# Pairs of tiles behind the early ones in three mixers, alternating pieces in the recurrent mixer, and pieces set apart from their chains

## The chip, the cores and the metric

The kernel runs on one core of one Trainium2 chip. Times are device microseconds (us) of one execution; several are taken and the median counts. Engines: PE is TensorE, DVE VectorE, ACT ScalarE, POOL GpSimd, SP the engine that issues the loads.

## The reference

A sequence of 256 tokens with 1024 features goes through six layers, in float32. The first two are hybrid layers: an input projection `w_in`, then three token mixers side by side (retention with rotated q and k, gated linear attention "gla" with its q called gq, and softmax attention with normalised q and k, "fox": fq, fk, fv), gated and summed, then a feed-forward part with a short convolution. The last four have one mixer each and a feed-forward part, with a normalisation behind each part. All norms are modulated by vectors from a condition `c` (scale, shift, gate: products of `c` with 288 blocks of 128 x 1024 weights).

```
def hybrid_layer(x, c_act, ...):
    h = modulate(rms_norm(x, norm1_g), shift1, scale1)
    (rq, rk, rv, rg, gq, gk, gv, glr, gg, fq, fk, fv, ff) = jnp.split(h @ w_in, split_points, axis=-1)
    ...
def second_block(x, c, ...):
    for i in range(4):
        h = x * (1 + scale[0]) + shift[0]
        y = (mlstm_mixer, swa_mixer, hgrn2_mixer, diff_mixer)[i](h, ...)
        x = layer_norm(alpha * x + (1 + gate[0]) * y, ...)
        h = x * (1 + scale[1]) + shift[1]
        x = layer_norm(alpha * x + (1 + gate[1]) * swiglu(h, ...), ...)
```

swa is attention in a window of 128 with 16 query heads of 64 and two key heads; hgrn2 a gated recurrence with 8 heads of 128; diff attention takes the difference of two softmaxes in each of 8 heads and then a norm over each head.

## The kernel before

Activations lie transposed: eight tiles x0 to x7 of 128 features by 256 tokens. Every weight block (128 x 128) and every activation tile is split into a rounded high part and a low part, and three matmuls (high by high, high by low, low by high) make one block product: lines L501 to L503 (`mm3`, 256 columns, output transposed) or L508 to L510 (`mm3n`, output in token order, up to 512 columns wide). These are called dense matmuls here. SP loads weights in pieces of 128 x 1024 in the order of use; for each, ACT makes the high part (the cast, L469) and DVE the low part (L470).

The list of matrices (`dense_specs`) sets what is multiplied in which order: `tiles` for `dense_T`, `chunks` for `dense_N`. In `dense_T` the first `group` output tiles, the early ones, run over k in step, while the norm of the layer before isn't finished: they use unnormalised inputs, and `fix` corrects their sums (L799 to L803) once the norm is known. The functions in `after` then make the normed inputs x0 to x7 (in the last layers three DVE operations, L1402, L1404, L1407, and one of ACT each). `evac(f, tile)` takes a finished tile out of PSUM and may push pieces: a list `fill` of short functions (scores, softmax, transposes, values of one head and so on), of which one or more run behind each dense tile (`step`; `mid` says how often inside one). `late` puts a piece behind a wait for a chain; a chain is an inverse square root on POOL (L653 to L664, L839). `held` pieces are kept back. What is issued to an engine stays in that order.

Where the matrices have a `second` number of tiles (up and fi, the feed-forward parts: groups of six, two pairs), these run behind the early tiles as pairs, again over k in step, and the inputs are made in two parts: x0 to x5, two fixes and evacuations, x6 and x7, the other fixes and evacuations.

Stages that the text names: up0, down0 (feed-forward of the first layer), rk1, gs1, fq1, fk1, fv1, gv1, gq1, rv1, rq1 (projections of the second hybrid layer), ml_* (mLSTM), sw_in and sw_w (sliding window), hg_qf0, hg_v, hg_qf1, hg_g, hg_w (hgrn), df_kq0, df_v0, df_kq1, df_v1, df_w (diff). `RATES` says how many modulation blocks are loaded by SP and summed by DVE (L415) per dense tile of a stage.

In hgrn the heads are worked in four pairs of twelve pieces each: `first` and five levels (L1799, matmuls of 32 x 32), three wide ones (L1842, L1852, L1857), `heads` (L1869 to L1871) with a chain on POOL, an empty one and `done`. In diff, heads 0 to 3 have pieces at once and 4 to 7 are held until the second half of the values exists; the piece `done` normalises a head and transposes it (L823).

## Time and profile before

| what | value |
|---|---|
| median of three runs | 2310.58 us (2307.93 to 2315.93) |
| profiled execution | 2307.1 us, span 2305.3 us |
| TensorE busy | 2198.5 us, 95% |
| VectorE busy | 1879.3 us, 82% |
| ScalarE busy | 1249.3 us, 54% |
| GpSimd busy | 104.8 us, 5% |
| mean granted TensorE clock | 0.981 of full speed |

The stages run one behind the other on PE. Busy time of PE contains overlap of matmuls in its pipeline, so a stretch is read by the idle time before an instruction and what ended it. The chain of work that ended last is PE for 48% and issue on PE for 36% of the span.

### The profile page before, as it was taken

How to read it: one execution, taken by the hardware profiler on the slowest of the kernel's cores; microseconds unless marked ns; L12 is line 12 of the kernel's file. 1: busy time of each engine (PE TensorE's matmuls, PEld its weight loads, DVE VectorE, ACT ScalarE, POOL GpSimd, SP SyncE). 2: the span in 40 equal slices, each digit the busy share in tenths (PEclk: the TensorE clock that was granted, in tenths of full speed). 3: DMA queues.
4: the chain of work that ended last, by engine and by line, in shares of the span. 5: the costliest groups of instructions: out<-in, count | busy, mean ns of one | idle time of the engine just before them, and what ended most of it. 6: DMA issues, size and time to landing. Idle time of an engine off the chain costs nothing.

```text
span 2305.3 us, 46019 instructions
## 1 busy us (share of the span) xinstructions
PE 2198.5 (95%) x17991; PEld 2104.0 (91%) x17991; DVE 1879.3 (82%) x3624; ACT 1249.3 (54%) x2426; POOL 104.8 (5%) x280
## 2 busy tenths in 40 slices
PE   6999999998999999989999999999989999889997
PEld 5899999996899999979999879998879999779997
DVE  8879898877877888847998869887769987968855
ACT  3545475454554665456644576445655544576542
POOL 0011000002020000002000000000010000030000
PEclk9999999999999999999999999999999999899998
DMA  9759858856777578945699325984545896444751
GB/s 358 254 177 341 280 197 266 310 190 235 254 250 274 186 249 276 328 151 174 209 374 324 109 92 170 326 308 156 170 135 173 310 317 212 140 132 144 258 184 34
DMA packets 144939, 520.26 MB, mean 226 GB/s; under 512 B 16208, under 2 KB 18512, under 8 KB 144720
## 3 DMA queue, kind: packets, MB, share of 16 engines
q1 hardware_dynamic: 144432, 517.15, 65.6%
q8 instruction: 141, 2.31, 0.4%
q14 instruction: 78, 0.64, 0.1%
q10 hardware_dynamic: 288, 0.16, 0.0%
HBM read 516.20 MB, written 1.05 MB: 224 GB/s over the span
## 4 chain that ended last, share of the span: by engine, by line
PE 48%; issue 36%; DVE 8%; POOL 3%; ACT 2%; DMA 2%; SPq 0%; POOLq 0%; ACTq 0%; DVEq 0%
PE dps L501 13%; PE dps L502 13%; PE dps L503 13%; DVE l L470 2%; POOL nr L656 2%; DMA w<-in_ada_dram 1%; PE dps L509 1%; PE dps L510 1%; PE dps L508 1%; DVE junk L415 1%; ACT h L469 1%; DVE t L1407 1%; PE mps L502 1%; ACT t L882 1%; PE mps L503 1%
## 5 line engine op out<-in xcount | busy, mean ns | idle before, releaser
L501 PE MATMUL dps<-t,h 128*128 128x256 f32 (+1 forms) x4664 | 1325.1, 285 | 6.9 <-DVE t L1259 3.2
L502 PE MATMUL dps<-t,h 128*128 128x256 f32 (+1 forms) x4664 | 1318.7, 283 | 2.1 <-DVE t L491 2.0
L503 PE MATMUL dps<-t,l 128*128 128x256 f32 (+1 forms) x4664 | 1315.3, 283 | 2.0 <-DVE l L470 2.0
L469 ACT CAST h<-w 128x1024 fp32r<-128x1024 f32 x689 | 718.2, 1047 | 627.6 <-PE dps L502 338.2
L470 DVE TENSOR_TENSOR l<-w,h 128x1024 fp32r<-128x1024 f32 x689 | 832.9, 1216 | 179.9 <-ACT h L469 175.4
L501 PEld LDWEIGHTS dps<-t,h 128*128 128x128 f32 x4664 | 883.4, 190 | 12.5 <-issue 6.5
L503 PEld LDWEIGHTS dps<-t,l 128*128 128x128 f32 x4664 | 885.2, 190 | 4.7 <-DVE l L470 2.9
L502 PEld LDWEIGHTS dps<-t,h 128*128 128x128 f32 x4664 | 884.6, 190 | 4.5 <-DVE t L491 2.6
L415 DVE SCALAR_TENSOR_TENSOR junk<-w,cb 128x1024 bf16<-128x1024 f32 x288 | 350.8, 1218 | 52.2 <-DMA w<-in_ada_dram 44.7
L508 PE MATMUL dps<-h,t 128*128 128x512 f32 (+2 forms) x288 | 107.6, 385 | 15.5 <-ACT t L882 6.1
L509 PE MATMUL dps<-l,t 128*128 128x512 f32 (+2 forms) x288 | 108.2, 381 | 4.7 <-DVE l L470 4.5
L510 PE MATMUL dps<-h,t 128*128 128x512 f32 (+2 forms) x288 | 106.8, 380 | 0.0
L490 ACT CAST t<-t 128x256 fp32r<-128x256 f32 x172 | 68.1, 403 | 58.4 <-DVE t L1265 25.8
L839 POOL TENSOR_SCALAR nr<-nr 128x2 f32<-128x2 f32 (+2 forms) x22 | 13.7, 624 | 1587.7 <-ACT junk L882 1544.8
L508 PEld LDWEIGHTS dps<-h,t 128*128 128x128 f32 x288 | 57.6, 201 | 28.6 <-ACT t L882 9.2
L502 PE MATMUL mps<-t,h 128*128 128x256 f32 (+1 forms) x288 | 81.0, 284 | 1.7 <-DVE t L1407 1.7
L501 PE MATMUL mps<-t,h 128*128 128x256 f32 (+1 forms) x288 | 80.2, 285 | 1.1 <-ACT t L882 1.1
L503 PE MATMUL mps<-t,l 128*128 128x256 f32 (+1 forms) x288 | 80.3, 284 | 0.9 <-DVE l L470 0.9
L491 DVE TENSOR_TENSOR t<-t,t 128x256 fp32r<-128x256 f32 x172 | 70.4, 417 | 5.9 <-ACT t L490 5.9
L509 PEld LDWEIGHTS dps<-l,t 128*128 128x128 f32 x288 | 57.7, 201 | 15.1 <-DVE l L470 7.3
L510 PEld LDWEIGHTS dps<-h,t 128*128 128x128 f32 x288 | 57.2, 201 | 8.8 <-issue 0.3
L502 PEld LDWEIGHTS mps<-t,h 128*128 128x128 f32 x288 | 54.4, 189 | 2.3 <-DVE t L1407 2.3
(387 smaller groups left out, 2075.4 us busy)
## 6 DMA issues: line engine op xcount, KB each, us to landing
w<-in_w_dram SPq DMA_DIRECT2D x683, 512.0 KB, 4.6
w<-in_ada_dram SPq DMA_DIRECT2D x288, 512.0 KB, 5.0
w<-in_w_dram SPq DMA_DIRECT2D x4, 414.0 KB, 4.1
t<-in_c_dram SPq DMA_DIRECT2D x4, 256.0 KB, 4.4
X<-in_x_dram SPq DMA_DIRECT2D x8, 128.0 KB, 3.6
v<-in_ret_dram SPq DMA_DIRECT2D x2, 512.0 KB, 7.7
out_dram<-X SPq DMA_DIRECT2D x8, 128.0 KB, 2.0
cols<-in_cols_dram SPq DMA_DIRECT2D x1, 740.0 KB, 6.8
```

What stands on the lines that cost most here:

```text
L415: self.nc.vector.scalar_tensor_tensor(out=self.junk, in0=w, scalar=0.5, in1=self.cb, op0=ALU.mult, op1=ALU.mult, accum_out=self.mod[l][:, ...
L469: nc.scalar.copy(h[:, q:e], raw[:, q:e]).ins,
L470: nc.vector.tensor_tensor(out=low[:, q:e], in0=raw[:, q:e], in1=h[:, q:e].bitcast(F32), op=ALU.subtract).ins]
L490: nc.scalar.copy(t[:, 0], src)
L491: nc.vector.tensor_tensor(out=t[:, 1], in0=src, in1=t[:, 0].bitcast(F32), op=ALU.subtract)
L501: mm(pt, lhsT=h, rhs=x[:, 0], start=first, stop=False)
L502: mm(pt, lhsT=h, rhs=x[:, 1], start=False, stop=False)
L503: self.last_mm = mm(pt, lhsT=low, rhs=x[:, 0], start=False, stop=last).ins
L508: mm(pt, lhsT=x[:, 0, sl], rhs=h, start=first, stop=False)
L509: mm(pt, lhsT=x[:, 0, sl], rhs=low, start=False, stop=False)
L510: self.last_mm = mm(pt, lhsT=x[:, 1, sl], rhs=h, start=False, stop=last).ins
L656: e.tensor_tensor(out=o, in0=a, in1=b, op=ALU.mult)
```

## The change

In the list of matrices, three mixers get a pair behind their four early tiles: rk1 takes gq1's two tiles as its pair (gq1's own stage goes), hg_qf0 and df_kq0 have six tiles instead of four (hg_qf1 and df_kq1 ten instead of twelve). In `dense_T` the two branches on the group's size become branches on `second`, and the `elif not norm` becomes `else`. In hgrn the pieces of a new pair of heads alternate with the last eight in the list; `gated` goes to the front of the list from the fourth tile of hg_g. In diff `done` is divided: the normalisation, and a stage later `rows` with the transposes; three heads are pushed at once. In mLSTM two transposes become a piece of their own (`as_columns`), and three empty pieces stand in front of the first head. In the second hybrid layer the normalisation pieces of q and k come two pieces later. Of the rates, up0 goes from 0.32 to 0.5, down from 3 to 2.2 (down0 to 2).

```diff
-            tiles(f"rk{l}", 8, 4, cols(slice(RK, RK + 512)))
+            tiles(f"rk{l}", 8, 6, cols(list(range(RK, RK + 512)) + list(range(GQ, GQ + 256))), 4, 2)
...
-    tiles("hg_qf0", 8, 4, lambda i: qf(i)[:, :512])
+    tiles("hg_qf0", 8, 6, lambda i: qf(i)[:, :768], 4, 2)
...
-    tiles("df_kq0", 8, 4, lambda i: kq(i)[:, :512])
+    tiles("df_kq0", 8, 6, lambda i: kq(i)[:, :768], 4, 2)
...
-RATES = dict(..., up0=0.32, down=3, ...
+RATES = dict(..., up0=0.5, down=2.2, down0=2, ...
...
-                if group == 4:
+                if not s["second"]:
                     xs = []
                     for f in range(group):
                         pts[f] = norm["fix"](pts[f])
                         xs += [t() for t in after[2 * f:2 * f + 2]]
                     for f in range(group):
                         evac(f, pts[f])
-            if norm and group > 4:
+            if norm and s["second"]:
                 xs = [t() for t in after[:6]]
                 self.fixes(norm, [0, 1], pts, evac)
                 xs += [t() for t in after[6:]]
                 self.fixes(norm, range(2, group), pts, evac)
-            elif not norm:
+            else:
                 for f in range(group):
                     evac(f, pts[f])
...
-            rk, hx = rotated(f"rk{l}", norm)
+            hx = self.dense_T(f"rk{l}", norm, lambda f, pt: ev_k(f, pt) if f < 4 else evac_gq(f - 4, pt))
...
-            self.fill += [norm_q]
+            self.fill += [lambda: None] * 2 + [norm_q]
...
-        self.fill = [lambda: None] * 3 + [lambda h=h: decay(h) for h in range(4)]
+        self.fill = [lambda: None, as_columns, lambda: None] + [lambda h=h: decay(h) for h in range(4)]
...
-                    self.fill += pieces(b)
+                    k = max(0, len(self.fill) - 8)
+                    new, alone, old = pieces(b), self.fill[:k], self.fill[k:]
+                    self.fill = alone + [p for a in zip(old, new) for p in a] + new[len(old):]
...
-        held, self.fill = self.fill[9:], self.fill[:9]
+        held, self.fill = self.fill[8:], self.fill[:8]
         self.dense_N("hg_v", hx, evac_v)
-        self.fill += held
-        self.mid = 2
+        self.drain()
+        self.fill = held
+        self.mid = 1
...
-            if f > 5:
-                gated()
+            if f > 2:
+                self.fill.insert(0, gated)
...
+        def rows(h, o):
+            t = o[0]
             out[h] = self.split(self.transposed(lambda th: t[:, th * 128:(th + 1) * 128]), lm[:, 3:4])
...
-            if h < 2:
+            if h < 3:
                 first.append(stages)
...
-        self.dense_N("df_v0", hx, evac_v)
+        self.fill = [lambda: None] * 3 + self.fill
+        self.dense_N("df_v0", hx, evac_v, 1)
```

Lines of the changed kernel lie 1 to 13 further down. DVE at the head of the differential mixer, before: the casts' low parts (l), the fix of the first two early tiles (L800, L802), and the inputs' operations (t2 is an input's low part).

```order
L470 TENSOR_TENSOR l_24593<-w_24590,h_24592 128x1024
L470 TENSOR_TENSOR l_24719<-w_24716,h_24718 128x1024
L470 TENSOR_TENSOR l_24725<-w_24722,h_24724 128x1024
L800 TENSOR_TENSOR t1_24621<-dps_24464,t2_24582 128x256
L1402 SCALAR_TENSOR_TENSOR t1_24627<-Z0_114,c4_23656,t2_24582 128x256
L802 SCALAR_TENSOR_TENSOR t1_24621<-t2_24582,nr_24620,t1_24621 128x256
L1404 SCALAR_TENSOR_TENSOR t1_24627<-t2_24582,c4_23656,t1_24627 128x256
L1402 SCALAR_TENSOR_TENSOR t1_24633<-Z1_115,c4_23656,t2_24582 128x256
L800 TENSOR_TENSOR t1_24639<-dps_24465,t2_24582 128x256
L1407 SCALAR_TENSOR_TENSOR t2_24626<-t1_24627,c4_23656,t2_24626 128x256
L1404 SCALAR_TENSOR_TENSOR t1_24633<-t2_24582,c4_23656,t1_24633 128x256
L802 SCALAR_TENSOR_TENSOR t1_24639<-t2_24582,nr_24638,t1_24639 128x256
```

The same place in the changed kernel:

```order
L471 TENSOR_TENSOR l_24712<-w_24709,h_24711 128x1024
L471 TENSOR_TENSOR l_24840<-w_24837,h_24839 128x1024
L1403 SCALAR_TENSOR_TENSOR t1_24740<-Z0_114,c4_23776,t2_24701 128x256
L1403 SCALAR_TENSOR_TENSOR t1_24746<-Z1_115,c4_23776,t2_24701 128x256
L1405 SCALAR_TENSOR_TENSOR t1_24740<-t2_24701,c4_23776,t1_24740 128x256
L1405 SCALAR_TENSOR_TENSOR t1_24746<-t2_24701,c4_23776,t1_24746 128x256
L1403 SCALAR_TENSOR_TENSOR t1_24752<-Z2_116,c4_23776,t2_24701 128x256
L1403 SCALAR_TENSOR_TENSOR t1_24758<-Z3_117,c4_23776,t2_24701 128x256
L1405 SCALAR_TENSOR_TENSOR t1_24752<-t2_24701,c4_23776,t1_24752 128x256
L1408 SCALAR_TENSOR_TENSOR t2_24739<-t1_24740,c4_23776,t2_24739 128x256
L1408 SCALAR_TENSOR_TENSOR t2_24745<-t1_24746,c4_23776,t2_24745 128x256
L1408 SCALAR_TENSOR_TENSOR t2_24751<-t1_24752,c4_23776,t2_24751 128x256
```

One cast fewer stands in front, and the fixes have gone from between the inputs. PE in hgrn, before: the last pieces of one pair of heads (L1857, L1869 to L1871, tiles t2_20248 and t2_20249) and the first of the next (L1799).

```order
L1857 MATMUL mps_20634<-t2_20248,t2_20249 128x128
L1857 MATMUL mps_20637<-t2_20248,t2_20249 128x128
L1869 MATMUL mps_20653<-v_19586,at0_19582 128x128
L1799 MATMUL mps_20717<-t2_20455,t2_20457 32x32 x8
L501 MATMUL dps_20736<-t2_19792,h_20739 128x256
L502 MATMUL dps_20736<-t2_19792,h_20739 128x256
L503 MATMUL dps_20736<-t2_19792,l_20740 128x256
L501 MATMUL dps_20736<-t2_19804,h_20739 128x256
L502 MATMUL dps_20736<-t2_19804,h_20739 128x256
L1870 MATMUL mps_20653<-v_19586,at0_19582 128x128
L1871 MATMUL mps_20653<-v_19587,at0_19582 128x128
```

In the changed kernel (L1858 is L1852, L1805 is L1799):

```order
L1858 MATMUL mps_20782<-t2_20004,t2_20005 64x64 x2
L1858 MATMUL mps_20787<-t2_20004,t2_20005 64x64 x2
L503 MATMUL dps_20794<-t2_19881,h_20797 128x256
L504 MATMUL dps_20794<-t2_19881,l_20798 128x256
L1805 MATMUL mps_20816<-t2_20525,t2_20527 32x32 x8
L502 MATMUL dps_20794<-t2_19887,h_20797 128x256
L503 MATMUL dps_20794<-t2_19887,h_20797 128x256
L504 MATMUL dps_20794<-t2_19887,l_20798 128x256
L502 MATMUL dps_20794<-t2_19913,h_20797 128x256
L1805 MATMUL mps_20817<-t2_20525,t2_20527 32x32 x8
L503 MATMUL dps_20794<-t2_19913,h_20797 128x256
```

The new pair's first piece now stands between the old pair's wide ones and not behind them. DVE at the head of the sliding-window mixer, before: the rotation of the early tiles t1_16016 and t1_16034, then of a later tile that comes straight from PSUM (dps).

```order
L1659 STREAM_SHUFFLE t1_16064<-t1_16016 128x256
L1660 TENSOR_TENSOR t1_16065<-t1_16016,rcos_1673 128x256
L1661 TENSOR_TENSOR t1_16064<-t1_16064,rsin_1672 128x256
L1659 STREAM_SHUFFLE t1_16070<-t1_16034 128x256
L1662 TENSOR_TENSOR t1_16065<-t1_16065,t1_16064 128x256
L1660 TENSOR_TENSOR t1_16071<-t1_16034,rcos_1673 128x256
L1661 TENSOR_TENSOR t1_16070<-t1_16070,rsin_1672 128x256
L1659 STREAM_SHUFFLE t1_16110<-dps_16076 128x256
L1662 TENSOR_TENSOR t1_16071<-t1_16071,t1_16070 128x256
```

The changed kernel, where the early tiles are t1_15960, t1_15996 and t1_16014:

```order
L1663 STREAM_SHUFFLE t1_16050<-t1_16014 128x256
L1666 TENSOR_TENSOR t1_16045<-t1_16045,t1_16044 128x256
L1664 TENSOR_TENSOR t1_16051<-t1_16014,rcos_1672 128x256
L1665 TENSOR_TENSOR t1_16050<-t1_16050,rsin_1671 128x256
L1663 STREAM_SHUFFLE t1_16056<-t1_15960 128x256
L1666 TENSOR_TENSOR t1_16051<-t1_16051,t1_16050 128x256
L1665 TENSOR_TENSOR t1_16056<-t1_16056,rsin_1671 128x256
L1664 TENSOR_TENSOR t1_16057<-t1_15960,rcos_1672 128x256
L1416 TENSOR_TENSOR X3_89<-Z3_117,t2_15921 128x256
L1666 TENSOR_TENSOR t1_16057<-t1_16057,t1_16056 128x256
L1417 TENSOR_TENSOR X3_89<-X3_89,t2_15921 128x256
L1663 STREAM_SHUFFLE t1_16069<-t1_15996 128x256
```

The tile t1_15960 is shuffled and rotated here again; t1_16031 and t1_16032 were made from it 15 rows earlier, and only those rows stand in the kernel before.

## Rows read from the trace of the kernel before

**Rows 1.** The page, busy time of each engine, share of the span, instructions.

```profile
PE 2198.5 (95%) x17991; PEld 2104.0 (91%) x17991; DVE 1879.3 (82%) x3624; ACT 1249.3 (54%) x2426; POOL 104.8 (5%) x280
```

**Rows 2.** Busy us by stretch: PE, PEld, DVE, ACT, POOL; PEclk; DMA share, GB/s.

```profile
299.00:429.00 130.00, 126.75 (x1072) 126.17 (x1071) 113.08 (x206) 75.25 (x127) 0.00 (x0) 1.00 0.74 244
1286.00:1346.00 60.00, 56.06 (x373) 47.08 (x371) 50.02 (x167) 38.94 (x105) 0.00 (x0) 0.89 0.20 68
1627.00:1685.00 58.00, 51.03 (x768) 46.65 (x767) 42.08 (x80) 37.27 (x128) 7.22 (x24) 0.97 0.45 138
1685.00:1727.00 42.00, 36.93 (x462) 33.64 (x460) 27.13 (x60) 25.07 (x86) 7.77 (x24) 0.96 0.46 141
2061.00:2096.00 35.00, 28.63 (x214) 27.57 (x213) 18.92 (x39) 20.54 (x59) 11.25 (x48) 0.90 0.32 103
```

**Rows 3.** Timeline of PE in up0: start us, us, instruction, idle before and releaser.

```profile
410.39 0.36 PE L501 MATMUL dps<-t,h 128*128 128x256 f32 x1 [1.68 <-DVE t L1259]
```

**Rows 4.** Timeline of PE in the recurrent mixer (hgrn).

```profile
1649.35 0.51 PE L1799 MATMUL mps<-t,t 128*32 128x32 f32 x32 [2.47 <-DVE t L1819]
...
1662.02 0.45 PE L1842 MATMUL mps<-t,t 128*32 128x32 f32 x16 [0.41 <-DVE t L1810]
...
1678.16 0.46 PE L1799 MATMUL mps<-t,t 128*32 128x32 f32 x32 [2.23 <-DVE t L1810]
...
1699.50 0.46 PE L1799 MATMUL mps<-t,t 128*32 128x32 f32 x32 [2.88 <-DVE t L1810]
...
1725.96 0.44 PE L823 MATMUL mps<-const,t 128*128 128x128 f32 x2 [1.26 <-DVE t L1915]
```

**Rows 5.** Timeline of PE in the differential mixer (diff); last two: df_w.

```profile
1963.87 0.58 PE L508 MATMUL dps<-h,t 128*128 128x256 f32 x1 [2.19 <-ACT t L882]
...
1984.81 0.58 PE L509 MATMUL dps<-l,t 128*128 128x256 f32 x1 [2.67 <-DVE l L470]
...
2065.75 0.33 PE L823 MATMUL mps<-const,t 128*128 128x128 f32 x1 [1.14 <-ACT t L882]
...
2077.65 0.48 PE L823 MATMUL mps<-const,t 128*128 128x128 f32 x1 [2.24 <-ACT t L882]
```

**Rows 6.** Timeline of PE in the second hybrid layer.

```profile
507.05 0.39 PE L508 MATMUL dps<-h,t 128*128 128x276 f32 x1 [0.84 <-ACT t L814]
...
520.52 0.79 PE L508 MATMUL dps<-h,t 128*128 128x512 f32 x1 [3.09 <-ACT t L1014]
...
548.50 0.66 PE L973 MATMUL mps<-const,t 128*128 128x128 f32 x4 [1.42 <-DVE t L968]
...
559.60 0.63 PE L973 MATMUL mps<-const,t 128*128 128x128 f32 x4 [2.65 <-DVE t L968]
```

**Rows 7.** Timeline of DVE at the head of the differential mixer.

```profile
1958.21 3.49 DVE L470 TENSOR_TENSOR l<-w,h 128x1024 fp32r<-128x1024 f32 x3
...
1972.70 0.87 DVE L1404 SCALAR_TENSOR_TENSOR t<-t,c,t 128x256 f32<-128x256 f32 x2
```

**Rows 8.** Timeline of POOL, then of DVE, in df_w.

```profile
2071.68 1.59 POOL L656 TENSOR_TENSOR nr<-nr 128x2 f32<-128x2 f32 x3
...
2075.87 0.74 POOL L656 TENSOR_TENSOR nr<-nr 128x2 f32<-128x2 f32 x3
...
2071.69 1.25 DVE L470 TENSOR_TENSOR l<-w,h 128x1024 fp32r<-128x1024 f32 x1 [3.12 <-ACT h L469]
```

**Rows 9.** Timeline of PE in the sliding-window mixer: one head at full clock.

```profile
1359.95 0.23 PE L1693 MATMUL mps<-masks 128*128 128x128 bf16 x1
...
1363.41 0.36 PE L501 MATMUL dps<-t,h 128*128 128x256 f32 x1
...
1365.01 1.14 PE L1738 MATMUL mps<-t,t 128*64 128x128 f32 x12
1366.08 0.88 PE L1729 MATMUL mps<-const,t 128*128 128x128 f32 x6
```

**Rows 10.** The page's groups: busy us, mean ns, idle before, releaser: modulation sums.

```profile
L415 DVE SCALAR_TENSOR_TENSOR junk<-w,cb 128x1024 bf16<-128x1024 f32 x288 | 350.8, 1218 | 52.2 <-DMA w<-in_ada_dram 44.7
```

More of the change, by code (lines that the diff above doesn't have):

```diff
@@ L102, in dense_specs @@
                 chunks(f"{n}{l}", win, at, 512)
-        tiles(f"gq{l}", 8, 2, cols(slice(GQ, GQ + 256)), 0)
+        if not l:
+            tiles(f"gq{l}", 8, 2, cols(slice(GQ, GQ + 256)), 0)
         chunks(f"rv{l}", win, RV, 512)
@@ L926, in hybrid, with turned @@
         nc = self.nc
-        def rotated(name, xs):
+        def turned():
             out = []
@@ L987, in evac_to, with evac_gq @@
             return f
+        (ev_k, rk), (ev_q, rq), gq = turned(), turned(), []
+        def evac_gq(f, pt):
+            if f == 0:
+                gq.append(self.t2([128, 2, S]))
+            nc.scalar.mul(gq[0][:, f], pt, 64 ** -0.5)
+            if f and not l:
+                self.rest_of_inputs()
         fv, gv = [], []
@@ L1128, in hybrid @@
         if not l:
-            rk, _ = rotated(f"rk{l}", hx)
-        rq, _ = rotated(f"rq{l}", hx)
+            self.dense_T(f"rk{l}", hx, ev_k)
+        self.dense_T(f"rq{l}", hx, ev_q)
         self.drain()
@@ L1479, in mlstm, with as_columns @@
         ac = self.pc.tile([128, 2, 36], F32, name="mlac")
-        for th in range(2):
-            pt = self.mps()[:, :36]
-            nc.tensor.transpose(pt, rows[0:36, th * 128:(th + 1) * 128], ident[0:36, 0:36])
-            nc.vector.tensor_copy(ac[:, th], pt)
+        def as_columns():
+            for th in range(2):
+                pt = self.mps()[:, :36]
+                nc.tensor.transpose(pt, rows[0:36, th * 128:(th + 1) * 128], ident[0:36, 0:36])
+                nc.vector.tensor_copy(ac[:, th], pt)
         E = {}
@@ L1916, in gated @@
             out.append(self.split(z))
+        self.mid = 2
         self.dense_T("hg_g", hx, evac_g)
@@ L1999, in evac @@
             stages = ((lambda: scores(h, t, pp)), (lambda: weights(pp)), (lambda: turned(pp)),
-                      (lambda: values(h, pp, o)), (lambda: None), self.late(lambda: done(h, o)))
-            if h < 2:
+                      (lambda: values(h, pp, o)), (lambda: None), self.late(lambda: done(h, o)),
+                      (lambda: rows(h, o)))
+            if h < 3:
                 first.append(stages)
```

26 lines of the change are left out of this document (10 added, 16 removed).

## Prediction

> **What bounds the kernel now.** I read the page first: TensorE is busy 95% of the span, VectorE 82%, ScalarE 54% [rows 1]. So TensorE sets the time, and a stage that the change touches is worth what TensorE waits there, plus what its clock loses. Second, the busy times of the touched stretches [rows 2]: in each the reader is to compare the stretch's length with PE's share and to look at PEclk. In the feed-forward stretch 299 to 429 us 1072 matmuls of 256 columns take 130.0 us, or (130.0 - 1.68) / 1072 = 0.119 us each without the one wait of [rows 3]; I count 0.118. Third, PE's own waits in order of time, with what ended each [rows 3 to 6]. The clock is 0.89 to 0.97 of 2.4 GHz in the stretches that hold the long waits and 1.00 in the first, which has short ones: time at 1.2 GHz follows waits, and (1 - 0.97) x 58 = 1.7 us is what it costs in one such stretch.
>
> **The change part by part.** The sum is made against the profiled execution (2307.1 us).
>
> *Alternating pairs of heads (recurrent mixer, "hgrn").* Nothing is computed more or less; the pieces of a pair of heads (L1799 and so on) are dealt out between the last eight of the pair before. Now, the first pieces of a new pair come right behind the evacuation of its tiles, and PE waits 2.47, 2.23 and 2.88 us for ScalarE and VectorE to make their inputs [rows 4]. Then they come 15 dense matmuls later (15 x 0.118 = 1.8 us), which cover 1.8 of each: 5.4 us less. Four waits of some 0.4 us (one is the row of 0.41) go for the same reason (-1.7), and the time lost at the low clock behind the longest waits (0.03 x 58 and 0.04 x 42 us in [rows 2], 1.7 us each: -3.4). Against it: the last pair has nothing to alternate with. Its `done` needs a chain on GpSimd, and only 41 dense matmuls (4.8 us) stand in front of the transposes that read it, against a wait of 1.26 us now [rows 4]: I charge +1. The pair of tiles at the mixer's head gains nothing: the inputs x0 to x5 come sooner, x6 and x7 later (below), and I take 0. Sum -9.5; ends -4 (only the covered 1.8 us of two waits) and -13.
>
> *The pair behind the early tiles (differential mixer, "diff").* VectorE makes the mixer's eight inputs with three operations each, 0.40 us apart; three casts of 1.15 us stand in front [rows 7]. PE waits 2.19 us for the first input and 2.67 us for a cast's low half that is queued behind the rotations [rows 5]; from 1961 to 1985 us it finishes 55 dense matmuls and two heads' scores. In the new order two casts stand in front, then six inputs without the four tiles' evacuations between them, then two evacuations, then x6 and x7. By the durations of [rows 7] the casts are through at 1959.4 us, a cast and a sum earlier than now, and x0 is ready 3.2 us later, x5 8.4, x6 17.7. PE would wait about 1.5 + 2.2 us over x0 to x5, 36 matmuls of the pair and 36 of df_v0 run, then some 3.5 us for x6. At 1985 us it has done 57 to 72 dense matmuls more and one head's scores (1.2 us) less: -5.5 us. At the mixer's end the change loses: the four chains on GpSimd run one behind the other, PE waits four times, 1.14 to 2.24 us [rows 5], 6.4 us idle in that stretch [rows 2]. Those chains start when the last values exist, as before, but 51 instead of 67 dense matmuls now stand ahead of the last transposes: 16 x 0.118 = +1.9. Sum -3.6, taken as -3.5, ends -6 and +1.
> Five modulation sums (L415) also move into df_w; four come behind the last chain. While one cast of 1.25 us runs on VectorE, three GpSimd operations take 1.59 us where the same three take 0.74 without it [rows 8]: one sum in the way is +0.9 us, inside these ends.
> The Trainium skill, "SBUF — State Buffer", section "Who interferes with whom", says that a VectorE instruction with two SBUF inputs and a GpSimd instruction that reads SBUF share one read interface and that the later one is blocked. This case's rows agree (0.85 us longer). By that rule all five sums could hit the chains, which would make the sum below some 3.4 us worse than with one.
>
> *The pair in the hybrid layer's second pass.* gq's two tiles (48 matmuls, 5.7 us) move up behind rk's early ones. Before, PE waits 0.84 us at gs1 and 3.09 us for a ScalarE copy that needs a VectorE operation behind 14 rotations, then runs at half clock [rows 6]. After, x0 to x5 feed 36 + 36 matmuls; by the same walk x6 comes at about 518 us, 3.5 us after they are through. So a wait of about the same size stays, but 48 matmuls more are done at 528 us: -5.7, and -1.2 for the waits of gq's own stage. Of the waits for the normalised q and k, 1.42 and 2.65 us [rows 6], the second gets all of fv's 48 matmuls as cover (-2.6), the first loses 4 matmuls (+1). I leave 2.5 us for what the rotations then delay: -6, ends -10 and -1.
>
> *The branch on `second`.* The code that evacuates the early tiles stood under `elif not norm`; it now stands under `else`. In the sliding-window mixer, the one with a norm and no second pair, the four early tiles are therefore evacuated twice: k is rotated and v transposed again, and the first two pairs of heads' pieces are pushed twice. The order shows it: 42 matmuls more on PE than before in all, and every rotation of these tiles twice. One head costs PE 3.46 us for scores and transposes (1359.95 to 1363.41) and 1.07 us for values (1365.01 to 1366.08) [rows 9], so 4.5 us; two heads +9. PE is busy 56 of 60 us there [rows 2], so hardly any of it can hide: the low end is 6.5. The high end is 15: ScalarE gets some 7 us and VectorE some 7 us more at the mixer's head, where the clock is already 0.89.
>
> *Rates of the modulation sums.* 288 sums of 1.22 us; VectorE waits 44.7 us for their loads [rows 10]. up0 gets 17 loads instead of 11 and spreads its sums, down0 gets fewer. PE's wait of 1.68 us for VectorE behind a clustered three [rows 3] and a like one should go: -2. But VectorE is busy 113 of 130 us there [rows 2] and five more sums add 6: ends -4 and +2.
>
> *mLSTM.* The transposes that become columns of their own piece, and the three empty pieces, leave PE's order the same but for one head's scores 13 matmuls later: 0, ends -2 and +1. The other layers' order is unchanged.
>
> Sum: -9.5 - 3.5 - 6 + 9 - 2 + 0 = -12.0, so 2295.1 us in the profiled execution's terms. That execution lies 3.5 us under the median of the runs shown (2310.58), so I forecast a median of 2298.6 us, 0.5% faster. Within 0.3% of 2310.58, about what a measurement of this kernel can tell from no change, is 2303.6 to 2317.5.
>
> **Rivals.**
> 1. *The doubled heads eat the gain.* If the sliding-window mixer turns from PE to the chain of ScalarE and VectorE, with the low clock kept, each extra head costs its chain, not its matmuls: +18 instead of +9. For it: clock 0.89 there, ten pieces of heads left over for the end instead of six. Against it: ScalarE has 21 us free of 60 [rows 2]. 2307.6 us: no change.
> 2. *The waits only move.* Alternating pieces still hang on the same VectorE, ScalarE and GpSimd chains, so PE meets them at `heads` and `done`. Then hgrn gives -2, diff 0, hybrid -3, and the sum is -2 + 0 - 3 + 9 - 2 = +2: 2312.6 us, no change. For it: the chains on GpSimd are untouched [rows 8]. Against it: the waits of [rows 4] are for VectorE operations of some 2.5 us, not for GpSimd.
> 3. *x6 and x7 come too late, slower.* Behind x5 stand two fixes, two evacuations and up to four casts, each cast waiting for ScalarE's. My sum has PE wait 3.5, 0.7 and 3.5 us for x6 in three mixers. If each becomes the whole 9 us of that walk, the three cost 27 instead of 7.7, and three clock drops 5.1: 2298.6 + 24.4 = 2323.0. It decides from 12 us of further waiting. Against it: 36 matmuls of the next matrix (4.3 us, twice that where they have 512 columns) stand in front of x6 in all three.
> 4. *The change doesn't do all it says.* In mLSTM PE's order hardly moves; that is in the sum as 0. If the alternation, too, left PE's waits where they are, hgrn gives 0 and the sum -2.5: 2308.1.
>
> **How the numbers follow.** Forecast as worked out, or better, 0.59; rival 1 0.14, rival 2 0.12, rival 3 0.10, rival 4 0.05. Of the forecast 0.06 lies above 2303.6, of rivals 1 and 4 some 0.05 below it; of rival 2 some 0.03 above 2317.5, of rival 3 0.02 below it: 0.58 faster, 0.31 same, 0.11 slower. The ends of the parts add, by squares, to about 8 us: 2290 to 2307; rivals 1, 2 and 4 must be in: 2287 to 2313.
>
> **What would show it.** In the changed profile: the three waits of L1799's successor under 1.3 us and clock 1.00 between 1640 and 1690 us; the stretch from sw_in to sw_w some 9 us longer, with 42 more small matmuls; the wait for the differential mixer's first input under 1.6 us, one of 3 to 4 us for x6, and the four waits in df_w together 2 us longer; up0 without a wait over 1 us. It is wrong if the hgrn stretch (1580 to 1753 us) is not at least 6 us shorter, or the sliding-window one over 15 us longer.

## The result: slower by half a per cent

| | before | after |
|---|---|---|
| median | 2310.58 us (2304.45 to 2315.93) | 2320.42 us (2316.30 to 2328.96) |
| ratio to before, 95% interval | | 1.0054 [1.0031, 1.0077] |
| profiled execution, span | 2307.1, 2305.3 us | 2319.3, 2317.5 us |
| mean granted TensorE clock | 0.981 | 0.980 |

The forecast was 2298.6 us; the time lies above its whole range. The page of the kernel after, busy time by engine, answers [rows 1]: PE has 62 matmuls and 10.6 us more. All 62 stand in the sliding-window mixer (759 instead of 697); the prediction had counted 42.

```profile
PE 2209.1 (95%) x18053; PEld 2111.0 (91%) x18053; DVE 1886.5 (81%) x3657; ACT 1257.5 (54%) x2460; POOL 102.7 (4%) x280
```

The busy time by stretch answers [rows 2], in the same order of stages (up0, sw_in, the two halves of hgrn's later part, df_w); the last row is the stretch of gg1 and rg1 in the second hybrid layer. Columns: us, busy us of PE, PEld, DVE, ACT, POOL with instructions, PEclk, DMA share, GB/s.

```profile
302.00:428.00 126.00, 126.00 (x1070) 126.00 (x1068) 119.17 (x219) 76.90 (x128) 0.00 (x0) 1.00 0.80 274
1284.00:1360.00 76.00, 69.09 (x413) 54.18 (x413) 63.30 (x206) 46.80 (x128) 0.00 (x0) 0.81 0.24 77
1647.00:1694.00 47.00, 42.15 (x621) 38.79 (x620) 31.20 (x61) 31.74 (x97) 5.93 (x20) 0.96 0.48 151
1694.00:1733.00 39.00, 35.47 (x546) 33.23 (x545) 33.55 (x76) 26.06 (x95) 4.59 (x17) 1.00 0.46 144
2068.00:2101.00 33.00, 25.39 (x183) 24.28 (x182) 17.85 (x41) 16.94 (x48) 11.25 (x48) 0.84 0.44 143
611.00:649.00 38.00, 34.17 (x279) 31.15 (x278) 29.48 (x51) 14.85 (x33) 5.50 (x12) 0.91 0.73 248
```

The second row is the loss: 76 us where before took 60, at a clock of 0.81. The last row is one that the prediction never looked at: before, the same stages take 30 us.

```profile
619.00:649.00 30.00, 30.00 (x280) 28.51 (x279) 20.98 (x34) 14.74 (x33) 5.49 (x12) 1.00 0.62 211
```

Stage by stage, from the first matmul of a stage to the first of the next on PE's timeline (us; "half" is the time at the lower clock level). The dense matmuls are counted in the order of the list of matrices, because in the kernel after PE runs ten matmuls of fi3 ahead of the last of df_w:

| stages | before | after | difference | forecast |
|---|---|---|---|---|
| first layer's projections and out | 284.2 | 287.0 (half 6.8) | +2.8 | 0 |
| up0, down0 | 194.1 | 189.8 | -4.3 | -2 |
| second hybrid layer, rk1 to rq1 | 125.8 (half 10.2) | 118.8 | -7.0 | -6 |
| gg1, rg1 | 30.2 | 38.4 (half 6.8) | +8.2 | 0 |
| mLSTM | 125.4 | 124.6 | -0.8 | 0 |
| sw_in, sw_w | 101.8 (half 13.7) | 120.2 (half 30.7) | +18.4 | +9 |
| hgrn | 172.5 (half 13.6) | 165.0 (half 6.8) | -7.5 | -9.5 |
| diff | 149.3 (half 23.9) | 155.4 (half 19.7) | +6.1 | -3.5 |
| fi3 | 130.2 | 130.0 | -0.2 | 0 |
| all others | 976.8 | 973.2 | -3.6 | 0 |

The total is +12.1 us, that of the spans 12.2. A stage of one execution has a spread. Two kernels below were profiled twice, one as e6 and e13, one as e7 and e14: hgrn took 172.3 and 169.2 us in the first, down1 63.7 and 66.0 in the second, and diff 156.5 and 156.7, then 152.8 and 154.1. So a stage is believed here where several kernels repeat it.

### The profile page after: what moved, and what is told of

The parts are those of the page before. It is cut to its first block, busy times and chain, and to the rows that moved or that the text cites. A ratio compares the mean times of both kernels' runs of the same rounds, so it can differ in the third digit from the quotient of the medians.

```text
span 2317.5 us, 46209 instructions
## 1 busy us (share of the span) xinstructions
PE 2209.1 (95%) x18053; PEld 2111.0 (91%) x18053; DVE 1886.5 (81%) x3657; ACT 1257.5 (54%) x2460; POOL 102.7 (4%) x280
## 4 chain that ended last, share of the span: by engine, by line
PE 47%; issue 37%; DVE 9%; POOL 3%; DMA 2%; ACT 2%; SPq 0%; POOLq 0%; ACTq 0%; DVEq 0%
PE dps L502 12%; PE dps L504 12%; PE dps L503 12%; DVE l L471 2%; DMA w<-in_ada_dram 2%; POOL nr L657 2%; PE dps L511 1%; PE dps L509 1%; PE dps L510 1%; DVE junk L416 1%; ACT h L470 1%; PE mps L504 1%; PE mps L503 1%; PE mps L1700 1%; DVE t L1408 1%
## 5 line engine op out<-in xcount | busy, mean ns | idle before, releaser
L416 DVE SCALAR_TENSOR_TENSOR junk<-w,cb 128x1024 bf16<-128x1024 f32 x288 | 351.1, 1219 | 46.4 <-DMA w<-in_ada_dram 42.2
L509 PE MATMUL dps<-h,t 128*128 128x512 f32 (+2 forms) x288 | 103.7, 368 | 3.1 <-ACT t L815 2.0
L511 PE MATMUL dps<-h,t 128*128 128x512 f32 (+2 forms) x288 | 104.2, 366 | 0.0
L503 PE MATMUL mps<-t,h 128*128 128x256 f32 (+1 forms) x336 | 94.8, 286 | 4.2 <-DVE t L1408 3.2
L491 ACT CAST t<-t 128x256 fp32r<-128x256 f32 x172 | 68.2, 403 | 55.5 <-DVE t L1266 19.7
L502 PE MATMUL mps<-t,h 128*128 128x256 f32 (+1 forms) x336 | 93.1, 287 | 5.3 <-ACT t L883 4.6
L504 PE MATMUL mps<-t,l 128*128 128x256 f32 (+1 forms) x336 | 93.1, 284 | 2.6 <-DVE l L471 2.5
L503 PEld LDWEIGHTS mps<-t,h 128*128 128x128 f32 x336 | 63.4, 189 | 6.5 <-DVE t L1408 5.3
L502 PEld LDWEIGHTS mps<-t,h 128*128 128x128 f32 x336 | 62.0, 188 | 7.7 <-ACT t L883 6.1
L504 PEld LDWEIGHTS mps<-t,l 128*128 128x128 f32 x336 | 62.9, 189 | 3.9 <-DVE l L471 3.8
```

What stands on the lines that cost most here:

```text
L416: self.nc.vector.scalar_tensor_tensor(out=self.junk, in0=w, scalar=0.5, in1=self.cb, op0=ALU.mult, op1=ALU.mult, accum_out=self.mod[l][:, ...
L491: nc.scalar.copy(t[:, 0], src)
L502: mm(pt, lhsT=h, rhs=x[:, 0], start=first, stop=False)
L503: mm(pt, lhsT=h, rhs=x[:, 1], start=False, stop=False)
L504: self.last_mm = mm(pt, lhsT=low, rhs=x[:, 0], start=False, stop=last).ins
L509: mm(pt, lhsT=x[:, 0, sl], rhs=h, start=first, stop=False)
```

## Experiments

Lines of kernels with the branch on `second` are those of the kernel after. Ratios are to the kernel before on the same chip, whose medians were 2307.5 (e1 to e4), 2311.2 (e5 to e8), 2309.8 (e9 to e12) and 2308.2 us (e13 to e15).

### The doubled evacuations

e1 is the kernel after without them; e2 is the kernel before with them alone; e3 doubles only the heads' tiles, e4 only k's and v's.

```diff
e1_no_double (on after)
-            else:
+            elif not norm:
e2_double_alone (on before)
-            elif not norm:
+            elif not norm or name == "sw_in":
e3_double_heads (on after)
-                for f in range(group):
+                for f in (range(2, group) if norm else range(group)):
e4_double_kv (on after)
-                for f in range(group):
+                for f in (range(2) if norm else range(group)):
```

> The changed kernel with the one branch put back under `elif not norm`, so that the sliding-window mixer takes its four early tiles out once. The changed kernel spends 120.2 us between the start of sw_in and the start of fi1, before 101.8: 18.4 us more, of which two heads' matmuls are 9. Theory A (the doubled work costs all 18.4, half of it as low clock): that stretch falls back to 102 us (+-2), the other stages stay, and the median falls by 16 to 19 us under the changed kernel's, to about 2303, 0.3% under before. Theory B (the low clock there comes from elsewhere, for instance from where the stretch now starts, and only the two heads' matmuls go): stretch 111 us, median about 2311.

> The kernel before with nothing changed but the doubling: the sliding-window mixer's four early tiles are taken out twice. Theory A: the stretch from sw_in to fi1 is 120 us (+-2) instead of 101.8, and no other stage moves by more than 2 us. Theory B: 111 us.

> The changed kernel with only the two early tiles of queries taken out twice (their rotations and the pieces of two heads), k and v once. Tells which half of the doubling keeps the clock low. If the heads' small matmuls do it: stretch 117 to 120 us, half clock some 30 us. If the second transposition of v does it (PE waits 2.52 us for it in the changed kernel at 1316 us, and the clock falls there): 109 to 111 us, half clock some 14 us as before.

> The counterpart: only k's rotation and v's transposition are done twice, the heads once. If v's transposition brings the wait and the low clock: stretch 106 to 111 us, with a wait of 2 to 3 us at the second pair of transposes. If the heads bring them: 102 to 104 us.

Measured: e1 2304.43 us, ratio 0.9982 [0.9970, 0.9994]; against the kernel after that is 0.7%, some 16.6 us. sw_in and sw_w together take 102.3 us in e1, 118.7 in e2, 117.2 in e3 and 103.8 in e4 (e2 to e4 as a whole 2322.6, 2313.4 and 2306.2 us, one execution each). So the doubled evacuations cost 16 to 18 us wherever they stand, and most of it is the heads (14.9 us in e3), not k and v (1.5 in e4). How it comes to twice the price of the heads' matmuls is seen in the busy time by stretch of the kernel after, inside sw_in:

```profile
1300.00:1316.00 16.00, 13.77 (x98) 13.01 (x97) 16.00 (x49) 9.96 (x18) 0.00 (x0) 0.89 0.03 13
1316.00:1347.00 31.00, 29.87 (x139) 20.09 (x140) 23.46 (x95) 20.16 (x72) 0.00 (x0) 0.67 0.11 35
```

and of e1, the part behind the same point of the program:

```profile
1304.00:1318.00 14.00, 13.02 (x99) 12.01 (x100) 14.00 (x42) 7.96 (x16) 0.00 (x0) 1.00 0.10 37
1318.00:1334.00 16.00, 14.46 (x61) 8.34 (x60) 12.82 (x52) 13.20 (x42) 0.00 (x0) 0.70 0.10 34
1334.00:1348.00 14.00, 14.00 (x94) 12.00 (x93) 10.19 (x43) 9.39 (x34) 0.00 (x0) 0.85 0.12 39
```

In the first pair VectorE is busy all the time: 16.00 of 16 us against 14.00 of 14, with 49 instructions instead of 42, the doubled rotations. Then PE waits, on its timeline in the kernel after, 2.52 us for the second copy of v (L1752), which it is to transpose again:

```profile
1316.30 0.44 PE L824 MATMUL mps<-const,t 128*128 128x128 f32 x2 [2.52 <-ACT t L1752]
...
1353.39 1.15 PE L1742 MATMUL mps<-t,t 128*64 128x128 f32 x12 [1.39 <-ACT t L883]
```

Behind the 2.52 us PE is busy 29.87 of 31 us, but with 139 matmuls at a clock of 0.67. Time at the lower level is 30.7 us against 13.7, and (30.7 - 13.7) / 2 = 8.5 us is what that costs. With the two heads' own 9 us of the forecast it makes 17.5 of 18.4. In e2 and e3 the lower level lasts 23.9 us, so 5.1 us, which with the 9 makes 14.1 of 16.9 and of 14.9. PE's idle time in sw_in grew by 3 us (76 - 69.09 against 60 - 56.06); part of it lies in the time at the lower level and is in the 8.5 already, so the split is rough, but the larger share of what goes beyond the 9 us is matmuls that run slower.

The wait of 2.52 us is not what keeps the clock low: e4 has it too, on PE's timeline, and the clock stays at 1.00 behind it (second fence, the stretch around it), with 13.7 us at the lower level in all.

```profile
1318.92 0.44 PE L824 MATMUL mps<-const,t 128*128 128x128 f32 x2 [2.52 <-ACT t L1752]
```

```profile
1314.00:1328.00 14.00, 10.71 (x69) 6.95 (x68) 13.22 (x56) 12.46 (x35) 0.00 (x0) 1.00 0.01 2
```

So the doubled heads make the time at the lower level longer; by which step was not shown.

### The switch of the condition vector

The hybrid pair does what was forecast in its own stages (-7.0), and gg1 and rg1 lose 8.2 us right behind. Their PE waits in the kernel after:

```profile
615.81 0.36 PE L502 MATMUL dps<-t,h 128*128 128x256 f32 x1 [1.06 <-DVE t L938]
617.89 0.58 PE L502 MATMUL dps<-t,h 128*128 128x256 f32 x1 [1.60 <-ACT t L883]
620.43 0.58 PE L504 MATMUL dps<-t,l 128*128 128x256 f32 x1 [1.13 <-DVE l L471]
```

The modulation sums up to number 95 use one product of the condition (`cb`), the later ones a second that is loaded and computed in between. Where it is loaded hangs on the count of blocks that the stages before have loaded. The stage gq1 loaded one, and it is gone. SP's queue, before and then after (the two halves of the second condition):

```profile
578.53 0.38 SPq L340 DMA_DIRECT2D t<-in_c_dram  x1
582.08 0.38 SPq L340 DMA_DIRECT2D t<-in_c_dram  x1
```

```profile
581.37 11.82 SPq L460 DMA_DIRECT2D w<-in_w_dram  x2
...
596.64 0.38 SPq L341 DMA_DIRECT2D t<-in_c_dram  x1
...
599.53 0.42 SPq L341 DMA_DIRECT2D t<-in_c_dram  x1
```

It comes 17 to 18 us later. Modulation blocks that already lie in the buffers `w` can't be summed without it, so they keep the buffers, and a pair of weight loads takes SP 11.82 us (that the one is the reason for the other is my reading of the queue). ScalarE's timeline in the kernel after has the effect:

```profile
613.53 1.05 ACT L470 CAST h<-w 128x1024 fp32r<-128x1024 f32 x1 [4.09 <-DMA w<-in_w_dram]
```

The sums then come in a bunch: VectorE works 29.48 us in the stretch of gg1 and rg1 instead of 20.98, 8.5 us or seven sums of 1.22 us more. Two kernels tell this apart from what else the change does: e5, the kernel before with the hybrid part alone, and e7, e1 with one block more to load in gv1 (e14 is e7's kernel, timed).

```diff
e7_switch_earlier, e14_switch_earlier_timed (on e1)
-             gv1=1.25, fv1=4, ...
+             gv1=2.25, fv1=4, ...
```

> The kernel before with the second hybrid layer's part alone (gq's two tiles as rk's pair, the later normalisation pieces). In the changed kernel the stages rk1 to rq1 take 118.8 us instead of 125.8, and gg1 and rg1 38.4 instead of 30.2. Theory A (the part itself pays for its gain: gq's own stage also loaded one modulation block, and without it the switch to the second condition vector, which the sums from number 96 on wait for, comes one stage later, with up to seven loaded blocks holding weight buffers): both numbers appear here, 119 and 38 us, sum 157 as before's 156. Theory B (gg1 and rg1 are late because of the rates or the doubling): 119 and 30 us.

> The changed kernel without the doubling, and with one modulation block more loaded in gv1 (rate 2.25 instead of 1.25), so that the switch to the second condition comes where it was before. Theory A: gg1 and rg1 fall from 38.8 to 30 to 31 us, rk1 to rq1 stay at 119 to 120, nothing else moves by over 3 us; some 2296 us. Theory B (those stages are late because the pair moved work into them): they stay at 38 to 39 us.

> The changed kernel without the doubled evacuations and with gv1=2.25, timed; without gv1=2.25 it took 2304.4 us (0.9982 of before). Theory (the switch of the condition vector costs some 8 us in gg1 and rg1, and about 3 us at the low clock in down1 behind it): ratio 0.990 to 0.994, median 2289 to 2297. Rival (only the 7.8 us of gg1 and rg1): ratio 0.995 or above.

Measured: gg1 and rg1 take 38.5 us in e5 (one execution, 2313.9 us; rk1 to rq1 121.4 there, where 119 was expected) and 31.0 in e7 (one execution, 2289.0 us); rk1 to rq1 119.2 in e7, so the gain stays. e14: 2296.04 us, ratio 0.9949 [0.9932, 0.9965], against 0.9982 without the block: 7.6 us. That is the 7.8 us of the two stages; the further 3 us in down1 that the theory hoped for are not shown, and e7's single execution was a short one. Busy time of e14 in gg1 and rg1:

```profile
608.00:639.00 31.00, 31.00 (x283) 29.04 (x283) 26.97 (x46) 14.30 (x31) 5.51 (x12) 1.00 0.78 267
```

The clock is 1.00 again, and PE never idles.

### The rates

e6 is the kernel before with the new rates alone; e13 is the same kernel, timed. e8 is e14's with the down stages' rate as before, e11 with up0's as well.

```diff
e6_rates_alone, e13_rates_alone_timed (on before)
-RATES = dict(..., up0=0.32, down=3, ...
+RATES = dict(..., up0=0.5, down=2.2, down0=2, ...
e8_repaired (on e14)
-RATES = dict(..., up0=0.5, down=2.2, down0=2, ...
+RATES = dict(..., up0=0.5, down=3, down0=2, ...
e11_old_rates (on e8)
-RATES = dict(..., up0=0.5, down=3, down0=2, ...
+RATES = dict(..., up0=0.32, down=3, ...
```

> The kernel before with the changed rates alone. Theory A (the lower rate of down1 leaves too few loads, and four are forced in at df_v1, whose sums then stand on VectorE at the end of df_w, ahead of the low parts that the next stage waits for): up0 126 us instead of 129.9, but fi3 133 us instead of 130.2, with a PE wait of some 3 us for a low part; df_w at or above its 34.8 us. Theory B (that wait comes from the new order of the differential mixer): up0 126, fi3 130 us. For down1, which varied between 63 and 67.5 us in the kernels with these rates: the same spread is expected here, 63 to 67.

> The kernel before with the changed rates alone (up0=0.5, down=2.2, down0=2), timed, since two profiles of one and the same code differed by 3.8 us in the differential mixer. Theory (up0 gains 3.8 us; the four loads that are forced into df_v1 and the sums in df_w give back more): median 3 to 7 us above before's, fi3 133 us. Rival (the profiled 2315.2 us was mostly spread between executions): median within 2 us of before's or below.

> All parts of the change, with the three faults taken out: no doubling, one block more in gv1, and down1's rate back at 3 (down0 at 2, up0 at 0.5 as changed). If the three causes are the right ones, the stages show up0 126, rk1 to rq1 119, gg1 and rg1 30, sliding window 102, hgrn 165 to 167, differential mixer 147 to 150, fi3 130 us: 2305 - 4 - 7 - 7 - 1 = 2286 us as span of the profiled execution (+-4), some 0.8% under before. If it stays within 0.3% of the kernel without the doubling (2304 us), the gaps only move, as rival 2 had it.

> The repaired kernel with the rates of up0 and the down stages as before (0.32, 3, no down0). Theory (the new rate of up0 is worth its 3.8 us in up0, and five of its six loads more are fetched from stages where VectorE's sums cost nothing): up0 129.9 instead of 126.1 us, the rest equal within 2 us, median 2297 to 2300. Rival (the sums only move, later stages give as much back): up0 129.9, fi3 130 instead of 132.3 and df shorter by 1 to 2, median 2293 to 2296.

Measured: e13 2315.52 us, ratio 1.0033 [1.0020, 1.0046], so the rates alone cost 7.6 us (e6: 2317.0, one execution). up0 gains 4.0 us in both. But the lower rate of the down stages leaves four loads for diff, which SP issues while PE is in df_kq1, and five sums run in df_w. DVE in the kernel after at the end of df_w: two of the sums (L416, 1.21 us each) stand between the operations that make the next stage's input Z.

```profile
2091.22 0.48 DVE L1361 SCALAR_TENSOR_TENSOR Z<-dps,mod,X 128x256 f32<-128x256 f32 x1 [1.64 <-PE dps L504]
2091.62 1.21 DVE L416 SCALAR_TENSOR_TENSOR junk<-w,cb 128x1024 bf16<-128x1024 f32 x1
...
2092.76 0.48 DVE L1361 SCALAR_TENSOR_TENSOR Z<-dps,mod,X 128x256 f32<-128x256 f32 x1
2093.16 1.21 DVE L416 SCALAR_TENSOR_TENSOR junk<-w,cb 128x1024 bf16<-128x1024 f32 x1
```

The low part of df_w's own last piece of weights is queued behind all that (DVE, first fence), and PE waits for it (second fence): it has run ahead into fi3, whose early matmuls are 258 columns wide, and behind the wait it goes on with df_w's, which are 256 wide. The third fence is the same wait in e13.

```profile
2104.79 1.22 DVE L471 TENSOR_TENSOR l<-w,h 128x1024 fp32r<-128x1024 f32 x1
```

```profile
2102.93 0.28 PE L503 MATMUL dps<-t,h 128*128 128x258 f32 x1
2106.06 0.54 PE L504 MATMUL dps<-t,l 128*128 128x256 f32 x1 [2.84 <-DVE l L471]
2106.40 0.42 PE L502 MATMUL dps<-t,h 128*128 128x256 f32 x1
...
2110.29 0.28 PE L504 MATMUL mps<-t,l 128*128 128x258 f32 x1
```

```profile
2096.74 0.39 PE L503 MATMUL dps<-t,l 128*128 128x256 f32 x1 [2.03 <-DVE l L470]
```

So the theory of e6 and e13 had the wait right and its place wrong: fi3 takes 130.3 us in both and 130.2 before. df_w takes 39.9 to 40.6 us in the eight kernels with five sums there and 34.8 to 36.3 in the nine with one or none, 4.5 us more. Its four waits for the chains are not the reason where the pair is in: 7.6 us in the kernel after and 7.5 in e8, with one sum (without the pair 8.3 in e13 and 6.4 before). Besides up0 (-4.0) and df_w (+5.2), e6 and e13 are longer than before by 2 us in the rest of diff and by 5.4 and 3.7 us in down1. But down1 takes 63.2 us in the kernel after, with the same rates, and 66.7 in e5 with the old ones, so its part in the 7.6 us is not shown to come from the rates.

e8 has one sum in df_w: 2294.80 us, 0.9931 [0.9917, 0.9945]. That is 4 us under e14's ratio, with intervals that overlap; its span, 2293.4 us, lies above the 2286 (+-4) that its theory gave. e11: 2293.12 us, 0.9932 [0.9916, 0.9948]. So the higher rate of up0 is worth nothing measurable in sum, though up0 took 126.1 in e8 and 128.1 in e11: here e11's rival was right. e8 beats both kernels.

### The differential mixer

e12 is the kernel before with this part alone, e9 is e8 without it. e10 is e8 with an empty piece more in front of `done` for the heads of the first half, e15 is e11 with the same.

```diff
e10_done_later (on e8), e15_later_old_rates (on e11)
-                      (lambda: values(h, pp, o)), (lambda: None), self.late(lambda: done(h, o)),
+                      (lambda: values(h, pp, o)), (lambda: None), (lambda: None), self.late(lambda: done(h, o)),
...
-                held.append(stages[3:])
+                held.append(stages[3:5] + stages[6:])
```

> The kernel before with the differential mixer's part of the change alone. Theory (its gain is given back inside the mixer): df_kq0 to df_w 148 to 152 us (149.3 before), the time within 3 us of before's. Rival (as predicted, a gain of 3.5 us that other parts of the change spoil): 145 to 147 us, the time 3 to 5 us shorter.

> The repaired kernel (no doubled evacuations, gv1=2.25, down=3, down0=2) with the differential mixer as it was before. Theory (the pair's gain at the mixer's head is real but is given back by waits for the chains later, and the tail of df_w is worse): stages df_kq0 to df_w take 149 us (150.8 with the new diff code, 149.3 before), fi3 130 us (132.3 with it), and the median is 2290 to 2294, at or below the 2294.8 of the repaired kernel. Rival (the diff part is worth its predicted 3.5 us and something else in the changed kernel hides it): df 152 us or more, median 2297 to 2300.

> The repaired kernel with one more empty piece between values and done in the differential mixer, for the heads of the first half only. Theory (ScalarE, which works in order, stands 4.9 and 3.8 us before done's scaling for GpSimd's chain, and PE then waits 3.15 and 2.86 us for what is queued behind it): ScalarE's waits for GpSimd in df_kq1 fall from 9.6 us to under 3, PE's two long waits there to under 1.5 each, and df_kq0 to df_w take 146 to 148 us instead of 150.8. Rival (VectorE's rotations or PE's own values are next in line): ScalarE's waits for GpSimd fall as well, but PE meets others of like size, df 150 to 153 us.

> The changed kernel without the doubled evacuations, with gv1=2.25, with the rates of before, and with one more empty piece in front of done in the differential mixer. Theory (the rates are worth nothing in sum, the later done is worth 3 to 7 us): median 2285 to 2290, df 144 to 147 us. Rival (the 143.9 us of the run with the rates kept was a lucky execution): median 2291 to 2295, df 147 us or more.

Measured, stages df_kq0 to df_w, us:

| | without the pair | with the pair |
|---|---|---|
| five sums in df_w | e6 156.5, e13 156.7 | after 155.4, e1 154.2, e3 154.2, e4 153.7, e7 152.8, e14 154.1 |
| one sum or none there | before 149.3, e2 149.9, e5 149.6, e9 152.0 | e12 147.5, e11 147.0, e8 150.8 |
| the same, `done` later | | e10 143.9, e15 144.0 |

The means give the pair -2.5 us in the first line and -1.8 in the second, and the sums +6.4 and +5.6 by column, of which df_w has 4.5. By whole times, e9 (2292.41 us, 0.9923 [0.9905, 0.9940]) can't be told from e8, and e12 (one execution, 2307.9 us) is 1.9 us under before. e9's stages went against the theory (152.0 us where 149 was expected, though fi3 took its 130.1) and its whole time with it; one profile of a stage with such a spread decided nothing there. By the means of the table my theory that the gain is given back whole was too dark, and the rival's -3.5 too bright; in the second line single kernels overlap (e8), so the pair's 2 us are less sure than the sums' 6.

e8 and e11 have the same code here, differ in the rates of the first layer, and take 150.8 and 147.0 us. ScalarE works in order, and `done` makes it wait for a chain on GpSimd; whatever is queued behind waits with it. ScalarE's two long waits in e8, and what PE meets:

```profile
2008.49 0.40 ACT L883 ACTIVATE t<-t,nr 128x128 f32<-128x128 f32 x1 [4.89 <-POOL nr L657]
...
2023.35 0.69 ACT L883 ACTIVATE t<-t,nr 128x128 f32<-128x128 f32 x2 [3.75 <-POOL nr L657]
```

```profile
2012.30 0.80 PE L1941 MATMUL mps<-t,t 64*128 64x128 f32 x4 [3.15 <-DVE nr L1963]
2026.94 0.44 PE L824 MATMUL mps<-const,t 128*128 128x128 f32 x2 [2.86 <-ACT t L1986]
```

In e11 PE's longest wait in df_kq1 is 1.8 us, although ScalarE waits almost as long for GpSimd in the mixer's middle (8.9 us in all against 9.6); so the 3.8 us are not the chains' length alone, and the rest of their cause stays open. How long the chain takes depends on what VectorE runs at that moment, as [rows 8] showed for another chain: in the kernel after the median of the 56 operations of this line in the mixer is 0.195 us and the longest 1.23; in e8 one takes 1.21, beside a cast that starts 0.03 us ahead of it (GpSimd's, then VectorE's timeline).

```profile
2019.40 1.21 POOL L657 TENSOR_TENSOR nr<-nr 128x2 f32<-128x2 f32 x1
```

```profile
2019.37 1.20 DVE L471 TENSOR_TENSOR l<-w,h 128x1024 fp32r<-128x1024 f32 x1
```

The Trainium skill, "SBUF — State Buffer", section "Who interferes with whom", has it that such a pair shares one read interface and that the later of the two is blocked; these two rows agree, down to 0.01 us in the length.

With `done` a piece later ScalarE waits less for GpSimd (3.9 us in all; under 3 was expected). The waits by releaser, ScalarE in the mixer's middle (us in total, times, longest), of e8, then e10:

```profile
ACT t L883 <- POOL nr L657: 9.6, 3, 4.9
```

```profile
ACT t L883 <- POOL nr L657: 3.9, 2, 2.5
```

PE's longest wait in df_kq1 falls to 0.7 us, and the mixer takes 143.9 us; in e15, with the old rates, it takes 144.0, so it was no lucky execution. e10: 2288.03 us, 0.9910 [0.9895, 0.9924]. e15: 2289.38 us, 0.9927 [0.9914, 0.9939]. The mixer's gain of 3 to 7 us is shown by the stages; in the whole times it is -0.2% from e8 to e10 and -0.05% from e11 to e15, which the intervals don't separate. e10 is the fastest kernel of the study, 0.9% under before.

## Why the prediction was wrong, step by step

**The doubled evacuations (+9, measured +18.4).** That the `else` doubles them was read rightly, and the heads' matmuls were priced rightly. The step that failed is the term's size: it left out the clock, though PEclk 0.89 stood in [rows 2]. A price taken from rows at full clock [rows 9] was put into a stretch that already ran 13.7 us at the lower level, and with the extra heads it ran 23.9 to 30.7 us there. Its reading that time at 1.2 GHz follows waits would not have told this (last section). The upper end (+15) came from ScalarE's and VectorE's added work and didn't hold either. Rival 1 named the low clock and the price, +18, and got 0.14; its total of 2307.6 us failed because the next two steps failed as well. That the mixer turns from PE to the chain of ScalarE and VectorE, as it had it, the rows don't show: PE's idle time grew by 3 us only. Its ground against, that ScalarE has 21 us free of 60, was no ground: it is VectorE that is full at the mixer's head (16.00 of 16 us).

**The hybrid pair (-6, measured -7.0, then +8.2 behind it).** The step "gq's two tiles move up" was worked through on PE, ScalarE and VectorE and not on SP, whose cost stood at nothing: gq1's own stage also loads a modulation block, and that count sets where the second condition vector is loaded. The order of SP's queue would have shown it. The rest of the step held: the waits of 3.09, 1.42 and 2.65 us [rows 6] are gone down to one of 0.45, and so are 10.2 us at the lower clock; x6 came late by 0.63 and 0.70 us, not 3.5. New are three waits for low parts in gv1, the longest 2.37 us.

**The rates (-2, measured +7.6 alone).** The gain in up0 was even larger (-3.8; no wait over 1 us is left there, as forecast). The failed step is the sentence that five sums in df_w cost 0.9 us inside the ends of diff. They cost df_w 4.5 us. The prediction priced what a sum does to the chains on GpSimd (0.9 us for one, 3.4 more for all five), and those waits hardly moved (7.6 us against 7.5 in e8). The four sums that come "behind the last chain" had no price: on VectorE they stand ahead of the next stage's inputs and of the low part of df_w's last weights, and PE waits 2.84 us for that. With them diff is 6.1 us longer in the kernel after, over its upper end of +1.

**hgrn (-9.5, measured -7.5).** The mechanism was right. The waits that answer [rows 4], on PE's timeline after:

```profile
1664.41 0.46 PE L1805 MATMUL mps<-t,t 128*32 128x32 f32 x32 [2.60 <-DVE t L1825]
...
1681.40 0.33 PE L1805 MATMUL mps<-t,t 128*32 128x32 f32 x16 [0.81 <-ACT t L883]
...
1697.86 0.33 PE L1805 MATMUL mps<-t,t 128*32 128x32 f32 x16 [1.54 <-DVE t L1816]
1700.88 0.46 PE L1805 MATMUL mps<-t,t 128*32 128x32 f32 x32 [0.94 <-DVE t L1816]
...
1739.71 0.63 PE L824 MATMUL mps<-const,t 128*128 128x128 f32 x4 [2.82 <-DVE t L1888]
```

One long wait stays (2.60), the others fall to 0.8 to 1.5 (two are over the 1.3 us that the prediction named as a sign), and the last one grows from 1.26 to 2.82, by 1.6 where I charged 1. Half of the time at the lower clock is gone (13.6 to 6.8 us), the 3.4 us that were forecast. The stretch is 7.5 us shorter, over the 6 that were to decide. No run has this part alone; the eleven kernels with it take 163.4 to 166.3 us in hgrn, the six without it 169.2 to 172.5, on the mean 6.0 more.

**diff (-3.5, measured -1.8 to -2.5 for the pair).** Mis-sized, inside its ends. At the head, the first input's wait is 1.47 us (forecast about 1.5) and x6's 1.96 (forecast some 3.5), the first two rows of PE's timeline after:

```profile
1970.18 0.50 PE L502 MATMUL mps<-t,h 128*128 128x256 f32 x2 [1.47 <-ACT t L883]
...
1984.54 0.51 PE L502 MATMUL mps<-t,h 128*128 128x256 f32 x2 [1.96 <-ACT t L883]
...
2022.88 0.39 PE L502 MATMUL dps<-t,h 128*128 128x256 f32 x1 [3.12 <-ACT h L470]
```

So the head gained what it should, or more. The loss is in the third row: in the middle PE waits 3.12 us for a cast. On ScalarE's timeline that cast stands behind a scaling that has waited as long for GpSimd:

```profile
2021.19 0.69 ACT L883 ACTIVATE t<-t,nr 128x128 f32<-128x128 f32 x2 [3.12 <-POOL nr L657]
2021.79 1.98 ACT L470 CAST h<-w 128x1024 fp32r<-128x1024 f32 x2
```

e10 shows that this was the bound there: I let PE's lead at 1985 us stand to the mixer's end, when the mixer's middle waits on GpSimd through ScalarE. The four waits in df_w, by contrast, grew by 1.2 us (6.4 to 7.6) where 1.9 was charged.

**mLSTM (0, measured -0.8)** stands; with or without its part the kernels take 122 to 130 us there. **The first layer's +2.8** has no cause in the change that I can find: its waits are the same and 6.8 us more ran at the lower clock; in the other kernels with that code it takes 283 to 287 us.

Rival 2 (the waits only move) is right for diff's middle and wrong for hgrn and the hybrid layer. Rival 3 (x6 and x7 too late) is refuted: no wait for them was over 2 us in any of the three mixers. It gave almost the right time for a wrong reason.

The parts, each by its best measurement (doubling 16.6 by e1, rates 7.6 by e13, hybrid 1.2, hgrn -6, diff -2, mLSTM 0), add to +17, against 9.8 by the medians and 12.2 in the profiles. Half of that difference lies in the rates: alone they cost 7.6 us, in the changed kernel 3.9 (0.9949 in e14, 0.9932 in e11; the intervals overlap). With the three faults taken off in turn (-16.6, -7.6, -3.9) e11 is left, 15.7 us under before by its ratio; by stages the gains make some 14 (hybrid -5.8 with gg1 and rg1, hgrn -6, diff -2). What is left open is the rest of the difference, the worth of up0's rate by itself, which lies within the measurement's spread, what the rates do to down1, and why the doubled heads keep the clock low for longer.

## What to carry to other kernels

When a stage disappears, look at everything it issued, on the load queue too: a count of loads that it carried can move a switch that later work hangs on. A price taken at the full clock can be half of what work costs in a stretch whose clock is already low in part: the two doubled heads, priced at 9 us, cost 15 to 18. And work put "behind the last chain" of a stage stands, on the same engine, ahead of the weights and inputs that PE needs next.

A lead that PE gains at the head of a mixer is kept only if what bounds its middle lets it: one empty piece, so that an in-order engine no longer stands before a slow chain, was worth 3 to 7 us in that mixer's profiles, where the pair of tiles was worth about 2.
